# Hybrid attention trunk: deferred steps counted by written pieces, new ranks for PSUM copies and exponentials, later memory operands, and tiles moved from the raw ring to the temporaries

## The chip, the cores and the metric

The kernel runs on one core of a Trainium2 chip. The metric is the device time of one execution in microseconds; less is better. The time before is the median of 3 runs, 1416.64 us (1414.54 to 1416.74).

The engines are named as the profile names them: PE does the matmuls (PEld loads their weights), DVE, ACT and POOL do the elementwise work, SP issues all DMAs. Each works through its own instructions in a fixed order; semaphores tie them together.

## The reference

Two layers of an encoder over 512 tokens of width 1024. Each layer adds three parts to x:

```python
def hybrid_mixer(h, w_in, rpb, q_norm, k_norm, w_out, rows, cos, sin):
    proj = h @ w_in
    na_q, na_k, na_v, g_q, g_k, g_v = jnp.split(proj, IN_SPLIT_POINTS, axis=-1)
    na_out = neighbourhood_attention(...)                       # 8 heads of 64, window 8 x 16, learned bias
    g_q = apply_axial_rope(rms_norm(g_q, q_norm), cos, sin)     # 8 query heads
    g_k = apply_axial_rope(rms_norm(g_k, k_norm), cos, sin)     # 2 key heads
    gqa_out = gqa_block_attention(g_q, g_k, g_v)
    return jnp.concatenate([na_out, gqa_out], axis=-1) @ w_out

for l in range(DEPTH):
    x = x + hybrid_mixer(rms_norm(x, norm_mix[l]), ...)
    x = x + memory_cross_attention(rms_norm(x, ...), rms_norm(mem, ...), ...)   # 4 heads, 256 memory tokens
    x = x + conv_ffn(rms_norm(x, norm_ffn[l]), ...)             # width 2816, depthwise conv of 3, SwiGLU
return rms_norm(x, norm_final)
```

The parts that matter here are the grouped-query heads: their queries and keys are normalised per head and rotated before the scores.

## The kernel before, in words

**Precision and weights.** Every product is done in three matmuls of split operands (`mm3`): a high part hi, rounded to the matmul's type, and the rest lo. A weight tile is loaded by SP into a ring `raw` (`N_RAW`, 3 buffers of 512 KB in all), cast by ACT to hi (L260), and subtracted by POOL, seldom DVE, to lo (L261); hi and lo have 4 buffers each (`N_W`). `get_w` writes these steps: when weight n is asked for, the casts up to n + 2 and the loads up to `N_RAW` beyond the last cast are written. A load waits on SP, in SP's order, until the subtraction that frees its buffer is done.

**Order.** PE and SP keep the order in which the program is written. ACT, DVE and POOL are ordered before the run by a list scheduler: each instruction has a rank, the running number at which it was written; of what is ready in the scheduler's own estimate the lowest rank goes first. `behind(n)` adds n to the rank: positive goes later, negative earlier. On the chip these orders are fixed. A tile is taken from its pool when the scheduler places its first writer, and given back after its last reader; a writer waits until a buffer is free.

**Weaving.** In the mixer a hand-written pipeline (`weave`) runs the attention units: scores in slot s, softmax scaling in s + 1, transposes in s + 2, values after that. Between them a `Filler` writes pieces of projections. A piece is what a generator writes up to its next `yield`: half a projection (12 matmuls of 128x512), a quarter of the values, half an output block. The order of the fillers is: projections of the neighbourhood heads (`NA_ORDER`), then `gqa_project` for k, head pairs 0 and 1, v, head pairs 2 and 3 (two pieces each, p1 and p2), then `out_na`, `memory_keys`, `memory_values`, `close_rows`. A second filler, `ms`, prepares the memory operands; `MEM_STEPS[s]` says how many of its steps are written in slot s of the grouped-query attention. Its first step loads the memory (`load_mem`, two DMAs), later ones compute its statistics in layer 0 (squares L524, reductions L525, L532), and then its scaled and split operands (L508 POOL, L509 ACT, L510 POOL), which `memory_keys` reads.

**Deferred steps.** `late(n, fn)` holds back a step until n ticks have passed. `Late.tick` runs after each written piece (also of `ms`), and, before the change, also when a generator has ended (`Filler.step`). A step deferred from outside a tick counts one more, for the tick that follows at once. The steps that matter are these:

- `gqa_rope` after p2 of a head pair or of k: ACT copies the product out of PSUM (`xs`, L797) and squares it (`sq`, L798), DVE makes `cc` (L799).
- `swap`, one piece later: SP moves the halves of the head dimension by four DMAs into `xr`; PE sums the squares (`pv`); DVE (L808, L811) makes v.
- `rotate`, one piece after that: POOL takes the power (L817), spreads it to the head's columns (L818, into `sq`), and rotates (L819, L820).
- `norm`, two pieces later: PE turns the spread row factors (`mm<-ident,t` in the trace).
- `split`: DVE multiplies (L830), and `split_q` or `split_k` (L623 ACT, L627 DVE for k; L641, L643 for q) write the operands of the scores; for k, `double` then copies each half to the other partitions by SP.
- in layer 0, `project_first` defers `evict`: PE repeats the row factors of the first norm (`spread`, after the power L389 on POOL), ACT copies them (L399), and the first three projections are split.
- `straddle` (five DMAs of value blocks) and `turn` (transposes of the grouped values) are deferred likewise.

**Buffers.** PSUM has 4 tiles "mm" for products, 2 "sc" for scores, 2 "tr" for transposes and statistics. The pool `tpool` has 10 tiles `t` of 2 KB a partition for temporaries: exponentials (`es`, two a unit), `th` and `tt` of the values (L747, L748), `xs`, `xr`, `sq`, `cc`.

Of the kernel before, what the change touches and what calls it, by code (L numbers as in the profile page):

```python
# [12 lines left out]
AF = mybir.ActivationFunctionType  # L13
ALU = mybir.AluOpType
# [4 lines left out]
P = 128  # L19
# [5 lines left out]
NB = S // P  # L25
KC = D // P
HD = 64
# [6 lines left out]
BIG = 3.0e38  # L34
# [3 lines left out]
WTYPE = [0, 1, 1, 2]  # L38
# [9 lines left out]
NA_FILL = 2650  # L48
GQA_FILL = [2300] * 16 + [3000] * 4
MEM_FILL = [1, 1, 1, 2, 1, 0, 0, 2, 0, 1, 2]  # L50
MEM_STEPS = [1, 0, 1, 1, 1, 1, 1, 1, 1] + [0] * 11
W_BEHIND, N_RAW, N_W, AHEAD, AHEAD_HELD, N_WARM, N_LATE, N_FIRST = 45, 3, 4, 2, 5, 10, 4, 3


class InOrder:
# [67 lines left out]
class Filler:  # L123
# [9 lines left out]
    def step(self, n):  # L133
        while n > 0 and not self.closed():
            try:
                self.gate = next(self.gens[0])
                n -= 1
            except StopIteration:
                self.gens.pop(0)
            self.late.tick()  # L140

    def run(self, ns):
        self.owed += ns
# [29 lines left out]
def encoder_kernel(ctx: ExitStack, tc: tile.TileContext, t: dict, out: bass.AP):  # L173
    nc = tc.nc
    PE, SP = Counted(tc, nc.tensor), InOrder(tc, nc.sync)
    late = Late()
    ACT_IN_ORDER = InOrder(tc, nc.scalar)
    ACT, DVE, POOL = Free(nc.scalar), Free(nc.vector), Free(nc.gpsimd)
# [2 lines left out]
    xpool = ctx.enter_context(tc.tile_pool(name="xpool", bufs=1))  # L181
    wpool = ctx.enter_context(tc.tile_pool(name="wpool", bufs=N_W))
    rpool = ctx.enter_context(tc.tile_pool(name="rpool", bufs=22))
    tpool = ctx.enter_context(tc.tile_pool(name="tpool", bufs=10))
    spool = ctx.enter_context(tc.tile_pool(name="spool", bufs=24))
    psum = ctx.enter_context(tc.tile_pool(name="psum", bufs=2, space=PSUM))

    @contextmanager
    def behind(n):


        at = tc.cur_priority
        tc.cur_priority = at + n
        yield
        tc.cur_priority = at
# [177 lines left out]
    ident = cpool.tile([P, P], F32, name="ident")  # L373
# [182 lines left out]
    for l in range(DEPTH):  # L556
# [4 lines left out]
        bias = [None] * 4  # L561

        def load_bias(p):
            bias[p] = [rtile((4, 256), F32) for _ in range(2)]
            for j in range(2):
                SP.dma_start(bias[p][j][:, 0:3, :], t["bias"][l, 2 * p + j])
# [53 lines left out]
        def split_k(pm, kt, near):  # L620
            rows = [(slice(64 * j, 64 * j + 64), slice(64 - 64 * j, 128 - 64 * j)) for j in range(2)]
            for k, (r, o) in zip(kt, rows):
                ACT.copy(k[r, 0], pm[r])  # L623
                if near:
                    ACT.copy(k[o, 0], pm[r])
            for k, (r, o) in zip(kt, rows):
                DVE.tensor_sub(k[r, 1], pm[r], f(k[r, 0]))  # L627
                if near:
                    DVE.tensor_sub(k[o, 1], pm[r], f(k[r, 0]))

            def double():
                for k, (r, o) in zip(kt, rows):
                    SP.dma_start(f(k[o]), f(k[r]))

            if not near:
                late(2, double)

        def split_q(pm, st):
            halves = [(st[:, j], slice(64 * j, 64 * j + 64), slice(64 - 64 * j, 128 - 64 * j)) for j in range(2)]
            for v, r, o in halves:  # L640
                ACT.copy(v[r], pm[r])  # L641
            for v, r, o in halves:
                DVE.tensor_sub(v[o], pm[r], f(v[r]))  # L643
# [35 lines left out]
        def na_scores(u):  # L679
            p, bp = divmod(u, 2)  # L680
            if bp == 0 and p + 1 < 4:
                load_bias(p + 1)
            qst, kst = qk["q", p], qk["k", p]
            sc = [ps_s().rearrange("p (i n) -> p i n", i=2) for _ in range(2)]
            for i in range(2):
                b = 2 * bp + i
                qs, ks = slice(b * P, b * P + P), slice(WIN[b], WIN[b] + 256)
                for j in range(2):
                    for part in range(2):
                        PE.matmul(sc[j][:, i, :], qst[j][:, qs], kst[2 * part + j][:, ks], start=part == 0, stop=part == 1)  # L690
            nmx, sums = small(4), small(4)
            es = [tmp((2, 256)) for _ in range(2)]
            for j in range(2):
                for i in range(2):
                    b = 2 * bp + i
                    col = slice(2 * j + i, 2 * j + i + 1)
                    DVE.tensor_tensor_reduce(
                        out=sc[j][:, i, :], in0=sc[j][:, i, :], in1=bias[p][j][:, WTYPE[b], :],
                        op0=ALU.add, op1=ALU.min, scale=-1.0, scalar=BIG, accum_out=nmx[:, col])
            for j in range(2):  # L700
                for i in range(2):
                    col = slice(2 * j + i, 2 * j + i + 1)
                    ACT.activation(es[j][:, i, :], sc[j][:, i, :], AF.Exp, bias=nmx[:, col], scale=-1.0,
                                   accum_out=sums[:, col])
            na[u] = es, sums

        def na_normalise(u):
# [51 lines left out]
        gq, gk, gvt, gtab, r2 = [None] * 4, [], [], [], []  # L759
# [33 lines left out]
        def gqa_rope(g, pm):  # L793

            gain = qkg[:, l, 0:1] if g != "k" else qkg[:, l, 1:2]
            xs, xr, sq, cc = tmp(), tmp(), tmp(), tmp()
            ACT.activation(xs, pm, AF.Copy, scale=gain)  # L797
            ACT.activation(sq, pm, AF.Square)  # L798
            DVE.scalar_tensor_tensor(cc, pm, gain, gtab[0][:, 0], op0=ALU.mult, op1=ALU.mult)  # L799

            def swap():
                for i in range(4):
                    SP.dma_start(xr[32 * i : 32 * i + 32], xs[32 * (i ^ 1) : 32 * (i ^ 1) + 32])
                pv = ps_t()
                for b in range(NB):
                    PE.matmul(pv[:, 2 * b : 2 * b + 2], sq[:, b * P : (b + 1) * P], pairs, start=True, stop=True)
                v = small(2 * NB)
                DVE.tensor_tensor(v.rearrange("p (b j) -> p b j", j=2), pv[:, 0 : 2 * NB].rearrange("p (b j) -> p b j", j=2),  # L808
                                  r2[0].unsqueeze(2).to_broadcast([P, NB, 2]), op=ALU.mult)

                DVE.tensor_scalar(v, v, *((1.0 / HD, EPS) if g == "k" else (1.0, EPS * HD)), op0=ALU.mult, op1=ALU.add)  # L811
                late(1, lambda: rotate(v))

            def rotate(v):
                r = small(2 * NB)
                with behind(-40):
                    POOL.tensor_tensor(r, v, mhalf[:, : 2 * NB], op=ALU.pow)  # L817
                    POOL.tensor_copy(sq.rearrange("p (b d) -> p b d", d=HD), r.unsqueeze(2).to_broadcast([P, 2 * NB, HD]))  # L818
                POOL.tensor_mul(xr, xr, gtab[0][:, 1])  # L819
                POOL.tensor_add(xr, cc, xr)  # L820
                late(3, norm)

            def norm():
                pr = ps_mm()
                for b in range(NB):
                    PE.matmul(pr[:, b * P : (b + 1) * P], sq[:, b * P : (b + 1) * P], ident, start=True, stop=True)
                late(1, lambda: split(pr))

            def split(pr):
                DVE.tensor_mul(pr, xr, pr)  # L830
                if g == "k":
                    gk.extend(rtile((2, S)) for _ in range(2))
                    split_k(pr, gk, False)
                else:
                    gq[g] = rtile((2, S))
                    split_q(pr, gq[g])

            late(2, swap)


        ga, gpt = {}, {}
# [146 lines left out]
        def na_quanta(s):  # L988
# [324 lines left out]
```

## Time and profile before

| | |
|---|---|
| median of 3 runs | 1416.64 us |
| profiled execution, its own time | 1417.6 us |
| its span, first to last instruction | 1415.8 us |
| mean granted PE clock | 0.987 |
| DMA: bytes, mean rate | 138.83 MB, 98 GB/s |
| SP waiting for POOL's lo (L261) | 1031.8 us, 193 times |

The profile is one execution. "Busy" is the time in which an engine had an instruction running. Lines such as "[3.54 <-DVE r L627]" mean that the engine was idle for 3.54 us before the instruction, and that the last thing it waited for was DVE's instruction of line 627 that writes an r tile. The granted clock is the share of full speed at which PE was let run. Line numbers are those of the kernel before. Between about 370 us and 690 us, and between about 1060 us and 1360 us, the kernel is in the feed-forward part of a layer.

### The profile page before, as it was taken

The numbers are of one execution on the slowest core, as the hardware profiler recorded it, in microseconds if no ns is written. First come the engines' busy times: TensorE is split into PE (matmuls) and PEld (weight loads), VectorE is DVE, ScalarE is ACT, GpSimd is POOL, SyncE is SP. The second block draws the span as 40 slices with busy tenths as digits, with TensorE's granted clock in tenths as the row PEclk, the third lists the DMA queues.
The fourth block names the chain that finished last, engine by engine and source line by source line (L and its number), as shares of the span: only waits on it lengthen the run. The fifth ranks groups of instructions, "written<-read, shape, count | busy, mean of one in ns | idle before, by whom it ended". The sixth has DMA issues, their size and how long they took to land. (4 is left out here: it accounts for less than half of the span.)

```text
span 1415.8 us, 19240 instructions
## 1 busy us (share of the span) xinstructions
PE 1364.5 (96%) x7092; PEld 1165.1 (82%) x7092; DVE 838.2 (59%) x1421; ACT 703.2 (50%) x1308; POOL 724.0 (51%) x541
## 2 busy tenths in 40 slices
PE   7998899999999999999999988999999999999997
PEld 6897789877888888888888866997788888888897
DVE  4665876454687178358446555744638843871874
ACT  5675677655443234234556655766555432432341
POOL 2357866734444444444635767657164444444452
PEclk8999999999999999999999999999999999999998
DMA  7552412322333333332446431223133333333221
GB/s 233 145 151 72 114 46 75 104 74 61 89 95 100 103 90 93 102 96 87 135 130 172 126 96 47 63 73 114 37 96 95 93 104 89 100 93 105 88 77 60
DMA packets 218174, 138.83 MB, mean 98 GB/s; under 512 B 5984, under 2 KB 211040, under 8 KB 218080
## 3 DMA queue, kind: packets, MB, share of 16 engines
q1 hardware_dynamic: 218080, 137.60, 34.1%
q8 instruction: 56, 0.92, 0.3%
q14 instruction: 38, 0.31, 0.1%
HBM read 125.00 MB, written 2.10 MB: 90 GB/s over the span
## 5 line engine op out<-in xcount | busy, mean ns | idle before, releaser
L261 POOL TENSOR_TENSOR lo<-raw,hi 128x1024 fp32r<-128x1024 f32 (+2 forms) x268 | 499.1, 1874 | 517.4 <-ACT hi L260 497.8
L76 PE MATMUL mm<-xg,hi 128*128 128x512 f32 x1984 | 620.1, 394 | 9.0 <-DVE r L627 7.1
L76 PEld LDWEIGHTS mm<-xg,hi 128*128 128x128 f32 x1984 | 371.2, 189 | 85.1 <-issue 7.4
L260 ACT CAST hi<-raw 128x512 fp32r<-128x512 f32 (+2 forms) x276 | 224.1, 836 | 339.2 <-PE mm L76 285.3
L76 PE MATMUL mm<-xg,lo 128*128 128x512 f32 x992 | 388.4, 392 | 0.0
L76 PE MATMUL mm<-r,hi 128*128 128x512 f32 (+1 forms) x1160 | 337.0, 374 | 2.7 <-DVE r L457 2.0
L76 PEld LDWEIGHTS mm<-r,hi 128*128 128x128 f32 x1160 | 210.8, 189 | 41.2 <-DVE r L457 2.8
L1137 DVE SCALAR_TENSOR_TENSOR t<-t,par,t 128x7 f32<-128x7 f32 (+1 forms) x352 | 203.8, 646 | 34.0 <-ACT t L1130 34.0
L76 PEld LDWEIGHTS mm<-xg,lo 128*128 128x128 f32 x992 | 187.9, 189 | 40.0 <-DVE lo L261 0.4
L76 PE MATMUL mm<-r,lo 128*128 128x512 f32 (+1 forms) x580 | 216.5, 373 | 0.0
L76 PEld LDWEIGHTS mm<-r,lo 128*128 128x128 f32 x580 | 109.6, 189 | 19.3
L463 POOL TENSOR_SCALAR t<-t,s 128x512 f32<-128x512 f32 (+1 forms) x112 | 66.9, 613 | 77.3 <-DVE s L863 35.6
L1122 DVE TENSOR_TENSOR t<-mm,rep 128x512 f32<-128x512 f32 x88 | 60.1, 687 | 77.3 <-PE mm L76 62.0
L1139 ACT ACTIVATE t<-t 128x512 f32<-128x512 f32 x44 | 27.9, 633 | 139.2 <-DVE t L1137 139.1
L1143 DVE TENSOR_TENSOR r<-t,r 128x512 fp32r<-128x512 f32 x44 | 90.5, 2057 | 7.4 <-ACT r L1142 4.3
L1166 DVE TENSOR_TENSOR xT<-xT,mm 128x512 f32<-128x512 f32 x32 | 21.9, 686 | 106.7 <-PE mm L76 106.7
L76 PE MATMUL sc<-r,r 128*128 128x256 f32 (+1 forms) x352 | 72.5, 337 | 3.6 <-DVE r L457 1.7
L63 PE MATMUL tr<-ident,t 128*128 128x128 f32 x456 | 63.1, 277 | 6.1 <-DVE s L532 1.8
L1130 ACT ACTIVATE t<-t,par 128x512 f32<-128x512 f32 x88 | 66.8, 806 | 2.4 <-DVE t L1122 2.4
L63 PEld LDWEIGHTS tr<-ident,t 128*128 128x128 f32 x456 | 53.9, 143 | 13.5 <-issue 4.1
L76 PE MATMUL mm<-r,r 128*128 128x256 f32 (+1 forms) x428 | 62.4, 298 | 0.0
L76 PEld LDWEIGHTS sc<-r,r 128*128 128x128 f32 x352 | 52.0, 192 | 9.9 <-ACT r L456 3.0
(134 smaller groups left out, 1544.7 us busy)
## 6 DMA issues: line engine op xcount, KB each, us to landing
raw<-in_w_up SPq DMA_DIRECT2D x88, 512.0 KB, 3.9
raw<-in_w_in SPq DMA_DIRECT2D x34, 512.0 KB, 5.2
raw<-in_w_down SPq DMA_DIRECT2D x32, 448.0 KB, 3.8
raw<-in_w_mem_kv SPq DMA_DIRECT2D x16, 512.0 KB, 4.1
raw<-in_w_down SPq DMA_DIRECT2D x16, 512.0 KB, 4.2
r<-in_bias SPq DMA_DIRECT2D x16, 384.0 KB, 6.2
r<-r SPq DMA_DIRECT2D x22, 256.0 KB, 4.1
raw<-in_w_out SPq DMA_DIRECT2D x8, 512.0 KB, 5.0
```

Source lines behind the costliest of these rows:

```text
L63: return lambda *a, **k: self.tc.keep_in_program_order(op(*a, **k))
L76: return self.tc.keep_in_program_order(self.engine.matmul(out, lhsT, rhs, **k))
L260: act.copy(hi[:, k], raw[:, k])
L261: (POOL if eng[0] == "P" else DVE).tensor_sub(lo[:, k], raw[:, k], f(hi)[:, k])
L463: eng.tensor_scalar(e, e, sums[:, col : col + 1], 1.0, op0=ALU.mult, op1=ALU.mult)
L1122: DVE.tensor_mul(u, us[side], ffn.rep)
L1130: ACT.activation(cc, u, AF.Identity, bias=par[:, l, CB + ch : CB + ch + 1], scale=w[1])
L1137: DVE.scalar_tensor_tensor(cc[:, dst], u[:, src], wi, cc[:, dst], op0=ALU.mult, op1=ALU.add)
L1139: ACT.activation(cs[0], cs[0], AF.Silu)
L1143: DVE.tensor_sub(acts[j][1], cs[0], f(acts[j][0]))
L1166: DVE.tensor_add(xT[m], xT[m], pm)
```

## The change

Six things are done.

- `Filler.step` ticks only when a piece was written, no longer when a generator has ended. The delays of the rotation are set anew: swap 2 to 1, norm 3 to 2. The other deferred steps keep their numbers.
- The three instructions that read the product in `gqa_rope` get a rank 20 lower (earlier).
- The reductions and exponentials of the neighbourhood scores get a rank 30 higher (later).
- `xr` is taken in `swap` and not in `gqa_rope`; the spread row factors get a tile of their own, `rows`, in `rotate`, and no longer overwrite `sq`.
- `tpool` has 12 tiles and not 10; the raw ring has 2 buffers and not 3.
- `MEM_STEPS` starts two slots later.

```diff
-MEM_STEPS = [1, 0, 1, 1, 1, 1, 1, 1, 1] + [0] * 11
-W_BEHIND, N_RAW, N_W, AHEAD, AHEAD_HELD, N_WARM, N_LATE, N_FIRST = 45, 3, 4, 2, 5, 10, 4, 3
+MEM_STEPS = [0, 0, 1, 0, 1, 1, 1, 1, 1, 1, 1] + [0] * 9
+W_BEHIND, N_RAW, N_W, AHEAD, AHEAD_HELD, N_WARM, N_LATE, N_FIRST = 45, 2, 4, 2, 5, 10, 4, 3
...
                 self.gate = next(self.gens[0])
                 n -= 1
+                self.late.tick()
             except StopIteration:
                 self.gens.pop(0)
-            self.late.tick()
...
-    tpool = ctx.enter_context(tc.tile_pool(name="tpool", bufs=10))
+    tpool = ctx.enter_context(tc.tile_pool(name="tpool", bufs=12))
...
             es = [tmp((2, 256)) for _ in range(2)]
+            with behind(30):
...
-            xs, xr, sq, cc = tmp(), tmp(), tmp(), tmp()
-            ACT.activation(xs, pm, AF.Copy, scale=gain)
-            ACT.activation(sq, pm, AF.Square)
-            DVE.scalar_tensor_tensor(cc, pm, gain, gtab[0][:, 0], op0=ALU.mult, op1=ALU.mult)
+            xs, sq, cc = tmp(), tmp(), tmp()
+            with behind(-20):
+                ACT.activation(xs, pm, AF.Copy, scale=gain)
+                ACT.activation(sq, pm, AF.Square)
+                DVE.scalar_tensor_tensor(cc, pm, gain, gtab[0][:, 0], op0=ALU.mult, op1=ALU.mult)
 
             def swap():
+                xr = tmp()
...
-                late(1, lambda: rotate(v))
+                late(1, lambda: rotate(xr, v))
 
-            def rotate(v):
+            def rotate(xr, v):
                 r = small(2 * NB)
+                rows = tmp()
                 with behind(-40):
                     POOL.tensor_tensor(r, v, mhalf[:, : 2 * NB], op=ALU.pow)
-                    POOL.tensor_copy(sq.rearrange("p (b d) -> p b d", d=HD), r.unsqueeze(2).to_broadcast([P, 2 * NB, HD]))
+                    POOL.tensor_copy(rows.rearrange("p (b d) -> p b d", d=HD), r.unsqueeze(2).to_broadcast([P, 2 * NB, HD]))
                 POOL.tensor_mul(xr, xr, gtab[0][:, 1])
                 POOL.tensor_add(xr, cc, xr)
-                late(3, norm)
+                late(2, lambda: norm(xr, rows))
...
-                    PE.matmul(pr[:, b * P : (b + 1) * P], sq[:, b * P : (b + 1) * P], ident, start=True, stop=True)
-                late(1, lambda: split(pr))
+                    PE.matmul(pr[:, b * P : (b + 1) * P], rows[:, b * P : (b + 1) * P], ident, start=True, stop=True)
+                late(1, lambda: split(xr, pr))
...
-            late(2, swap)
+            late(1, swap)
```

In `na_scores` the reductions and exponentials are only indented under `with behind(30)`; the rest of their code is the same.

More of the change, by code (lines that the diff above doesn't have):

```diff
@@ L692, in na_scores @@
             es = [tmp((2, 256)) for _ in range(2)]
[L693 to L704, printed above, removed]
+            with behind(30):
+                for j in range(2):
+                    for i in range(2):
+                        b = 2 * bp + i
+                        col = slice(2 * j + i, 2 * j + i + 1)
+                        DVE.tensor_tensor_reduce(
+                            out=sc[j][:, i, :], in0=sc[j][:, i, :], in1=bias[p][j][:, WTYPE[b], :],
+                            op0=ALU.add, op1=ALU.min, scale=-1.0, scalar=BIG, accum_out=nmx[:, col])
+                for j in range(2):
+                    for i in range(2):
+                        col = slice(2 * j + i, 2 * j + i + 1)
+                        ACT.activation(es[j][:, i, :], sc[j][:, i, :], AF.Exp, bias=nmx[:, col], scale=-1.0,
+                                       accum_out=sums[:, col])
             na[u] = es, sums
@@ L811, in swap, with norm, split @@
                 DVE.tensor_scalar(v, v, *((1.0 / HD, EPS) if g == "k" else (1.0, EPS * HD)), op0=ALU.mult, op1=ALU.add)
-                late(1, lambda: rotate(v))
-            def rotate(v):
+                late(1, lambda: rotate(xr, v))
+            def rotate(xr, v):
                 r = small(2 * NB)
+                rows = tmp()
                 with behind(-40):
                     POOL.tensor_tensor(r, v, mhalf[:, : 2 * NB], op=ALU.pow)
-                    POOL.tensor_copy(sq.rearrange("p (b d) -> p b d", d=HD), r.unsqueeze(2).to_broadcast([P, 2 * NB, HD]))
+                    POOL.tensor_copy(rows.rearrange("p (b d) -> p b d", d=HD), r.unsqueeze(2).to_broadcast([P, 2 * NB, HD]))
                 POOL.tensor_mul(xr, xr, gtab[0][:, 1])
                 POOL.tensor_add(xr, cc, xr)
-                late(3, norm)
-            def norm():
+                late(2, lambda: norm(xr, rows))
+            def norm(xr, rows):
                 pr = ps_mm()
                 for b in range(NB):
-                    PE.matmul(pr[:, b * P : (b + 1) * P], sq[:, b * P : (b + 1) * P], ident, start=True, stop=True)
-                late(1, lambda: split(pr))
-            def split(pr):
+                    PE.matmul(pr[:, b * P : (b + 1) * P], rows[:, b * P : (b + 1) * P], ident, start=True, stop=True)
+                late(1, lambda: split(xr, pr))
+            def split(xr, pr):
                 DVE.tensor_mul(pr, xr, pr)
```

## The prediction

> **What bounds the kernel now.** I read the page first, then the busy time by stretches, then what the tensor engine waited for, then the timeline of each engine around its longest waits.
>
> ```profile
> span 1415.8 us, 19240 instructions
> ```
> ```profile
> PE 1364.5 (96%) x7092; PEld 1165.1 (82%) x7092; DVE 838.2 (59%) x1421; ACT 703.2 (50%) x1308; POOL 724.0 (51%) x541
> ```
>
> PE is busy for 96% of the span. The change adds and removes no matmul, so it can win only inside the other 51.3 us and in time lost to a lower clock. The stretches (busy us of PE, PEld, DVE, ACT, POOL, then granted clock, DMA share, GB/s) say where that lies:
>
> ```profile
> 125.00:175.00 50.00, 41.26 (x221) 35.14 (x219) 34.93 (x54) 28.42 (x56) 38.20 (x43) 0.93 0.33 90
> 800.00:875.00 75.00, 61.39 (x323) 51.62 (x323) 41.13 (x82) 40.83 (x93) 56.84 (x62) 0.93 0.29 80
> 400.00:425.00 25.00, 25.00 (x112) 20.72 (x111) 20.61 (x26) 10.55 (x14) 10.77 (x6) 1.00 0.33 94
> ```
>
> The feed-forward part (third row) has no idle PE at all: 25.00 us for 112 matmuls, 0.223 us each. The two stretches where the grouped-query heads are projected, rotated and normalised, one per layer, lose 8.7 and 13.6 us to idle PE, and their clock of 0.93 costs about 0.07 x 50 + 0.07 x 75 = 8.8 us more. PE's waits (total us, times, longest) name the causes:
>
> ```profile
> PE mm L76 <- POOL t L818: 7.4, 3, 3.9
> PE mm L76 <- DVE r L627: 7.1, 2, 3.5
> PE tr L76 <- POOL s L389: 6.9, 4, 4.4
> PE tr L76 <- ACT t L798: 5.5, 4, 2.3
> ...
> PE tr L63 <- DVE s L532: 1.8, 1, 1.8
> ...
> PE tr L63 <- DVE xg L457: 1.8, 2, 1.2
> ```
>
> Every one of these except part of L389 belongs to a step that the change moves or ranks anew. I call the two pieces of a projection p1 and p2 (12 matmuls, 12 x 0.223 = 2.7 us each).
>
> **The change part by part.**
>
> *The counter.* Before, the end of a generator also ticks. A projection spans two pieces and one such end, so a delay that crosses an end is a piece shorter than it reads. The new delays (swap 2 to 1, norm 3 to 2) put swap and norm back where they were. What was not re-tuned really moves, by one piece: the first evict, split (delay 1 from norm), double and straddle (copies through SP), the turn of the values. Steps of the memory filler tick as well, so the first slot of the grouped heads loses one tick, and the norm of head pair 2 falls one piece (six matmuls) later.
>
> *Evict in layer 0* (term 1). It now runs before the first piece of the next projection:
>
> ```profile
> 32.38 2.08 PE L76 MATMUL tr<-ident,s 128*128 128x128 f32 x8 [4.36 <-POOL s L389]
> ```
> ```profile
> 44.24 1.12 PE L76 MATMUL sc<-r,r 128*128 128x256 f32 x8
> ```
> ```profile
> 26.39 4.95 POOL L261 TENSOR_TENSOR lo<-raw,hi 128x512 fp32r<-128x512 f32 x4 [5.30 <-ACT hi L260]
> 31.30 1.04 POOL L389 TENSOR_TENSOR s<-s,mhalf 128x4 f32<-128x4 f32 x1
> ```
> ```profile
> 41.57 0.69 DVE L629 TENSOR_TENSOR r<-mm,r 64x512 fp32r<-64x512 f32 x1
> ```
>
> PE stands still from 28.0 to 32.4 because the power on POOL sits behind four weight subtractions. After, p1 (2.7 us) fills that hole and the repeat follows it at 30.7 at the earliest. But the first scores then wait for the splits, which end 42.26 - 32.38 = 9.9 us after the repeat starts: 40.6 at the earliest instead of 44.24, a gain of 3.6; if POOL keeps its order, the repeat stays at 32.38 and the scores start at 42.3, a gain of 1.9. I take **3.0**, nearer the first, since with one raw buffer less the later of those subtractions come later than the power.
>
> *Split of k, and copies in front* (terms 2 and 3). At 129.07 PE wants a buffer of the "mm" ring (4) for the values' projection:
>
> ```profile
> 129.07 0.70 PE L76 MATMUL mm<-xg,hi 128*128 128x512 f32 x2 [3.54 <-DVE r L627]
> ```
> ```profile
> 123.84 1.15 ACT L260 CAST hi<-raw 128x512 fp32r<-128x512 f32 x2
> 124.87 0.53 ACT L715 ACTIVATE t<-t,s 128x256 f32<-128x256 f32 x1
> 125.28 0.69 ACT L797 ACTIVATE t<-mm,qkg 128x512 f32<-128x512 f32 x1
> 125.85 0.61 ACT L798 ACTIVATE t<-mm 128x512 f32<-128x512 f32 x1
> 126.33 1.17 ACT L623 CAST r<-mm 64x512 fp32r<-64x512 f32 x2
> 135.02 1.19 ACT L747 COPY t<-mm 64x512 f32<-64x512 f32 x2 [7.52 <-PE tr L63]
> ```
> ```profile
> 127.53 1.39 DVE L627 TENSOR_TENSOR r<-mm,r 64x512 fp32r<-64x512 f32 x2 [2.15 <-ACT r L623]
> 128.95 0.75 DVE L799 SCALAR_TENSOR_TENSOR t<-mm,qkg,r 128x512 f32<-128x512 f32 x1
> ```
>
> All four are held: by the product of head pair 1 (until L799, 129.7), by the row factors of k (until L627, 128.9), and by two value products whose copy L747 starts only at 135.02. After, L797 to L799 rank in front of L260 and can end near 123.84 + 0.7 + 0.6 + 0.75 = 125.9, and L799 is no longer queued behind k's split, which comes a piece later. PE, ready at 129.07 - 3.54 = 125.5, would stand 0.5 us with a semaphore's time instead of 3.54. Two layers: 7.1 - 1.0 = **6.1**, between 0 and 7.1. The cast put behind costs nothing as long as the weight buffers lead (below).
>
> The four waits on L798 (5.5 us) are the swap's matmuls arriving before the square, behind a cast of the weights. The two longest, one a layer, follow a projection with only the first scores between:
>
> ```profile
> 157.73 1.05 PE L76 MATMUL tr<-pairs,t 128*128 128x2 f32 x8 [1.79 <-ACT t L798]
> ```
> ```profile
> 847.08 1.05 PE L76 MATMUL tr<-pairs,t 128*128 128x2 f32 x8 [2.29 <-ACT t L798]
> ```
> ```profile
> 844.69 1.13 ACT L260 CAST hi<-raw 128x512 fp32r<-128x512 f32 x2
> ```
>
> Without the casts ahead, 1.13 each, 0.66 and 1.16 are left of them; the other two, 1.4 together, vanish: 5.5 - 1.8 = **3.7**. The exponentials ranked behind wait only where ACT has something else; their rows are read two slots later, some 20 us, which hides it.
>
> *Memory two slots later, own tile for the rows* (terms 4 and 5).
>
> ```profile
> 164.60 1.87 POOL L508 TENSOR_SCALAR r<-r,par 128x256 f32<-128x256 f32 x4
> 166.39 0.63 POOL L818 COPY t<-s 128x512 f32<-128x512 f32 x1
> ```
> ```profile
> 167.08 1.76 PE L76 MATMUL mm<-ident,t 128*128 128x128 f32 x8 [2.29 <-POOL t L818]
> ```
> ```profile
> 860.28 0.62 POOL L818 COPY t<-s 128x512 f32<-128x512 f32 x1
> ```
>
> POOL runs the memory's scaling (L508, four for 1.87 us, eight a layer) ahead of the copy L818 that PE waits for. Loaded two slots later, the memory is not there yet. Of the three waits I leave 0.4 each on two: 7.4 - 0.8 = **6.6**, between 2 and 7.4. The waits on L532 (the memory's own statistics) and on L457, 3.6 us, move to later slots with the work; I count half, **1.8**, between 0 and 3.6. The moved step takes its two loads past one weight load on SP, its squares and reductions to slots 4 and 5. It is needed here:
>
> ```profile
> 213.62 0.40 PE L76 MATMUL mm<-r,hi 128*128 128x256 f32 x2
> ```
>
> That is slot 10; the last operands are written in slot 9, one slot (5.5 us) before, so there is cover, but little.
>
> *Tiles of tmp, 10 to 12, later taken.* At 125 us the code wants 16 tiles before: 4 of exponentials, 3 of values, 2 of k, 3 of head pair 0, 4 of pair 1. After, k's rows are already free and pair 1 has no tile for the swap yet: 14. Where tiles lack, SP waits too:
>
> ```profile
> SPq L63 <- DVE t L748: 43.3, 5, 15.7
> ```
>
> I read this as the swap's DMAs standing up to 15.7 us for a tile that the values still hold, with raw loads and doublings behind them in the same queue. This is what keeps terms 2 and 4 from failing; I give it no time of its own.
>
> *Raw buffers 3 to 2, doubling and straddle a piece later* (price nothing). In the feed-forward part:
>
> ```profile
> 500.99 2.41 POOL L261 TENSOR_TENSOR lo<-raw,hi 128x1024 fp32r<-128x1024 f32 x1 [3.06 <-ACT hi L260]
> ```
> ```profile
> 510.74 1.05 ACT L260 CAST hi<-raw 128x1024 fp32r<-128x1024 f32 x1 [2.84 <-PE mm L76]
> ```
> ```profile
> raw<-in_w_up SPq DMA_DIRECT2D x88, 512.0 KB, 3.9
> ```
>
> The load that goes out when a subtraction ends (503.4) lands at 507.3. With three buffers it serves the third cast after, with two the second, at 510.74: 3.4 us to spare, and PE is three weights further behind. The doubling of k goes out one piece and one weight load later, some 5 us, and is read two projections later. Straddle and the other doublings pass no weight load, since that piece is a second half.
>
> *Clock* (term 6). Fewer and shorter holes give back most of the 8.8 us: **7.0**, between 0 and 8.8.
>
> [...]
>
> *Sum.* 3.0 + 6.1 + 3.7 + 6.6 + 1.8 + 7.0 = 28.2 us. Against it I set new waits: without L508's 3.7 us POOL has 34.5 us of work in some 41 us of the first stretch and 53.1 in some 64 of the second, 84% and 83% of an engine that works in a fixed order. Ten projections are left with a wait each; I take 0.8 us, a little over the mean of the residues above (0.5, 0.66, 1.16, 0.4), so 8 us. 28.2 - 8 = 20.2. The profiled execution took 1417.6 us (span 1415.8 and 1.8 around it): 1397.4; it lay 1.0 above the median of the runs, 1416.64, so I say **1397** for the runs.
>
> **The rivals.**
>
> *Tiles still bind.* 14 wanted is above 12, and the rows now need a tile of their own. For: L747 waited 7.52 us although ACT was free. Against: 6 short becomes 2 short. Terms 2, 3, 4 and 6 halve: 28.2 - 11.7 - 8 = 8.5 us, 1408 (1404 to 1414).
>
> *Nothing is given back.* The full 28.2: about 1388 (1381 to 1389). Against it, the 84%.
>
> *The change does not do what it says.* Ranks and delays only order instructions before the run; if each queue comes out in an order with the same last arrivals, the time is 1414 to 1419. Against it: at least evict and split move in PE's own order.
>
> *Slower: the raw ring starves.* Two buffers turn over in landing + cast + subtraction, L + 1.05 + 2.41 + 0.1; two weights last PE 2 x 24 x 0.223 = 10.7 us. From L = 7.1 us on, PE waits at every weight. At L = 8 it is 0.4 us for each of 136 weights, 54 us, less the 20 above: about 1450; in a mild form 1420 to 1450. For: the ring is the only thing that the change makes smaller. Against: L is 3.9.
>
> **How the numbers follow.** Forecast (1389 to 1404) 0.50; tiles bind 0.22; nothing given back 0.10; no effect 0.07; slower 0.11. A measurement of this kernel tells about 0.2%, 2.8 us, from no change. Faster by more: 0.50 + 0.22 + 0.10 = 0.82; within: 0.07; slower: 0.11. Leaving out the slower case, the unchanged one and the lowest end of the third case, the range is 1384 to 1414; the likeliest case alone has 1389 to 1404.
>
> **What would show it.** PE's wait on L627 gone or below 1 us each; the wait on L818 gone with no L508 before 175 us; the wait on L798 down to two of about 1 us; scores at 44.24 some 3 us earlier; clock 0.97 or more in both stretches; no PE wait on a weight's hi or lo, and 25.00 us of PE in the feed-forward rows. A wait on L818 of 2 us or more says that tiles bind. PE waiting for lo anywhere after the start, or a feed-forward row below 25.00, says that the raw ring was the price. New waits on the transposes' tiles in slots 4 to 9 would say that the memory only moved its waits.

## The result, and the profile after

The kernel after takes **1402.39 us** (median of 4 runs, 1401.19 to 1403.34); the kernel before took 1416.69 us on the same chip (4 runs). The ratio is 0.9899, 95% interval 0.9882 to 0.9916: faster by 14.3 us. The forecast was 1397 us, 1384 to 1414. The profiled execution took 1401.19 us, the lowest of the four, so the profiles differ by a little more than the medians: their spans by 1415.8 - 1399.2 = 16.6 us.

Line numbers from L747 on shift a little. The rotation's copy, square and cc (before L797 to L799) are L799 to L801; v (L808, L811) is L811, L814; power, spread and rotation (L817 to L820) are L821 to L824; the multiply L830 is L834; the values' copy L747 is L748 and their L748 is L749; the grouped exponential L857 is L861; the reciprocal L863 is L867.

From the page of after:

```profile
span 1399.2 us, 19213 instructions
```
```profile
PE 1358.8 (97%) x7092; PEld 1158.8 (83%) x7092; DVE 835.1 (60%) x1421; ACT 702.8 (50%) x1308; POOL 722.9 (52%) x541
```

PE's idle time fell from 51.3 to 1399.2 - 1358.8 = 40.4 us. Its busy time fell too, by 5.7 us for the same 7092 matmuls; the mean clock rose from 0.987 to 0.993, and I count the 5.7 us as its share. The stretches of after, with the columns of the prediction:

```profile
0.00:50.00 50.00, 45.60 (x245) 38.92 (x246) 29.92 (x56) 31.99 (x61) 15.29 (x20) 0.97 0.66 194
125.00:175.00 50.00, 42.98 (x242) 35.60 (x241) 35.74 (x61) 28.78 (x57) 35.97 (x38) 1.00 0.37 100
800.00:875.00 75.00, 68.64 (x383) 59.05 (x383) 48.66 (x93) 45.74 (x103) 57.64 (x65) 0.95 0.30 85
```
```profile
400.00:425.00 25.00, 25.00 (x112) 20.69 (x111) 21.41 (x28) 11.21 (x15) 11.39 (x5) 1.00 0.32 93
```

The stretches are fixed in time, so after has got further in each. The clock is 1.00 in the first mixer stretch (0.93 before) and 0.95 in the second; in the first 50 us PE is busy for 45.60 us (before: 42.37, at a clock of 0.90). The feed-forward row is full, as before. PE's waits of after (total us, times, longest):

```profile
PE tr L63 <- DVE r L457: 3.8, 2, 1.9
PE mm L76 <- DVE t L801: 2.9, 2, 1.4
PE tr L76 <- ACT t L800: 2.7, 2, 1.3
PE tr L76 <- POOL s L389: 2.5, 3, 1.0
PE tr L63 <- DVE xg L457: 2.3, 2, 1.7
...
PE tr L63 <- POOL r L508: 1.6, 1, 1.6
PE mm L76 <- DVE r L643: 1.4, 1, 1.4
...
PE tr L63 <- ACT mem_rep L539: 0.8, 1, 0.8
```

The wait on the spread copies (L818 before, 7.4 us) is gone, and so is that on k's split (L627, 7.1); in its place stands 2.9 on cc. The waits on the power L389 and on the square lost 4.4 and 2.8. The waits on the transposes' tiles (`tr L63`) have grown: 6.1 us on L457 where there were 1.8, and 2.4 on the memory's own L508 and L539 where there were 1.8 on L532.

### The profile page after: what moved, and what is told of

Same layout as the page of the kernel before. It is cut to its first block, busy times and chain, and to the rows that moved or that the text cites. A ratio compares the mean times of both kernels' runs of the same rounds, so it can differ in the third digit from the quotient of the medians.

```text
span 1399.2 us, 19213 instructions
## 1 busy us (share of the span) xinstructions
PE 1358.8 (97%) x7092; PEld 1158.8 (83%) x7092; DVE 835.1 (60%) x1421; ACT 702.8 (50%) x1308; POOL 722.9 (52%) x541
## 4 chain that ended last, share of the span: by engine, by line
PE 88%; DVE 4%; ACT 3%; issue 2%; POOL 1%; DMA 1%; SPq 0%; DVEq 0%; ACTq 0%; POOLq 0%
PE mm L76 80%; PE sc L76 3%; PE tr L63 3%; PE tr L76 1%; ACT hi L260 1%; DVE r L457 1%; DMA raw<-in_w_down 1%; POOL lo L261 0%; POOL r L261 0%; DVE xg L457 0%; DMA raw<-in_w_in 0%; DVE s L859 0%; ACT t L800 0%; ACT t L799 0%; DVE t L801 0%
## 5 line engine op out<-in xcount | busy, mean ns | idle before, releaser
L261 POOL TENSOR_TENSOR lo<-raw,hi 128x1024 fp32r<-128x1024 f32 (+2 forms) x268 | 499.6, 1876 | 507.9 <-ACT hi L260 476.3
L76 PE MATMUL mm<-xg,hi 128*128 128x512 f32 x1984 | 617.7, 393 | 4.3 <-DVE t L801 2.9
L76 PEld LDWEIGHTS mm<-xg,hi 128*128 128x128 f32 x1984 | 369.9, 189 | 80.1 <-DVE t L801 3.3
L260 ACT CAST hi<-raw 128x512 fp32r<-128x512 f32 (+2 forms) x276 | 224.5, 836 | 347.0 <-PE mm L76 288.4
L76 PE MATMUL mm<-xg,lo 128*128 128x512 f32 x992 | 387.7, 391 | 0.0
L76 PE MATMUL mm<-r,hi 128*128 128x512 f32 (+1 forms) x1160 | 336.1, 374 | 2.5 <-DVE r L457 2.0
L76 PEld LDWEIGHTS mm<-r,hi 128*128 128x128 f32 x1160 | 210.3, 189 | 41.2 <-DVE r L457 2.8
L76 PEld LDWEIGHTS mm<-xg,lo 128*128 128x128 f32 x992 | 187.1, 189 | 40.3 <-DVE lo L261 0.7
L76 PE MATMUL mm<-r,lo 128*128 128x512 f32 (+1 forms) x580 | 216.1, 373 | 0.0
L76 PEld LDWEIGHTS mm<-r,lo 128*128 128x128 f32 x580 | 109.3, 188 | 19.2
L463 POOL TENSOR_SCALAR t<-t,s 128x512 f32<-128x512 f32 (+1 forms) x112 | 66.3, 607 | 75.2 <-DVE s L710 38.2
L76 PE MATMUL sc<-r,r 128*128 128x256 f32 (+1 forms) x352 | 73.2, 339 | 4.4 <-DVE r L457 1.8
L63 PE MATMUL tr<-ident,t 128*128 128x128 f32 x456 | 62.8, 274 | 11.8 <-DVE r L457 3.8
L63 PEld LDWEIGHTS tr<-ident,t 128*128 128x128 f32 x456 | 52.4, 140 | 20.4 <-issue 7.9
L76 PE MATMUL mm<-r,r 128*128 128x256 f32 (+1 forms) x428 | 62.5, 297 | 0.1
L76 PEld LDWEIGHTS sc<-r,r 128*128 128x128 f32 x352 | 51.8, 191 | 10.6 <-ACT r L456 3.0
```

The costliest lines, as they stand in the source:

```text
L63: return lambda *a, **k: self.tc.keep_in_program_order(op(*a, **k))
L76: return self.tc.keep_in_program_order(self.engine.matmul(out, lhsT, rhs, **k))
L260: act.copy(hi[:, k], raw[:, k])
L261: (POOL if eng[0] == "P" else DVE).tensor_sub(lo[:, k], raw[:, k], f(hi)[:, k])
L463: eng.tensor_scalar(e, e, sums[:, col : col + 1], 1.0, op0=ALU.mult, op1=ALU.mult)
```

## The experiments

The runs below come from several chips, and each ratio is to runs of the kernel before on the same chip (medians 1416.18 to 1418.93 us). Two variants of after are told apart by their ratios only from about 0.003 on; where the text uses less, it is the place of a wait in the traces that decides.

### The parts alone, added to the kernel before

**Tiles** (with the smaller raw ring, as in after).

```diff
-... N_RAW ... = 45, 3, 4, ...      tpool bufs=10
+... N_RAW ... = 45, 2, 4, ...      tpool bufs=12
```

> The kernel before with 12 temporary tiles and 2 raw buffers, nothing else. My theory (tiles): the hole of 3.54 us ahead of the values' projection shrinks to about 1.4 us in both layers and part of the clock comes back, the waits on L818 stay: 7 us less, ratio 0.995 (0.993 to 0.997). Rival (the raw ring has a price): PE or the casts wait for weights, and the gain is eaten: 0.998 or more. Rival (order): the hole is set by the place of k's split and stays at 3.5 us: 0.998 to 1.002.

1407.74 us, ratio 0.9932 [0.9916, 0.9947]: 9.3 us, two thirds of the whole gain, with no rank, delay or step changed; the ring's own share is in the next run. The hole before the values' projection, 3.54 us in before, in this run:

```profile
125.48 0.73 PE L76 MATMUL mm<-xg,hi 128*128 128x512 f32 x2 [1.67 <-DVE t L799]
```

k's split no longer ends it; PE waits only until DVE has read the product of head pair 1. The copy of the value products, which started at 135.02 in before after 7.52 us of idle ACT, and SP's wait on the values' tiles, 43.3 us in before, are in this run:

```profile
126.04 1.19 ACT L747 COPY t<-mm 64x512 f32<-64x512 f32 x2
```
```profile
SPq L63 <- DVE t L748: 0.8, 2, 0.5
```

**The raw ring.**

```diff
-... N_RAW ... = 45, 3, 4, ...
+... N_RAW ... = 45, 2, 4, ...
```

> The kernel before with one edit: N_RAW 3 to 2 (the raw weight ring alone, 10 temporaries as before). It prices what the slower rival of the prediction blamed. Theory: the ring costs nothing, because a load lands in 3.9 us and the subtraction that frees the buffer runs well ahead of PE; 1415 to 1419 us, ratio 0.999 to 1.001, feed-forward windows at 25.00 us of PE. Rival: the ring has a price of its own, which the two more temporaries only paid back in the earlier runs; then 3 us or more over the kernel before, ratio 1.002 or more, with PE waits on lo or hi, or loads later in the mixer.

1417.51 us (12 runs; the profiled one, 1413.19, is the lowest), ratio 1.0011 [0.9999, 1.0022]. The smaller ring costs at most 0.2%. One PE wait on a weight shows, 0.7 us on a cast 5.2 us into the run; with three buffers e8_evict has one of 0.3 us. SP's wait on the values' tiles (L748) is 43.0 us here, so it is the tiles and not the ring that end it in e6_tmp12. POOL at the start, in this run:

```profile
26.27 2.50 POOL L261 TENSOR_TENSOR lo<-raw,hi 128x512 fp32r<-128x512 f32 x2 [5.54 <-ACT hi L260]
28.74 1.02 POOL L389 TENSOR_TENSOR s<-s,mhalf 128x4 f32<-128x4 f32 x1
```

Before, four subtractions (4.95 us) stood ahead of the power; now two do, and it starts 2.6 us earlier. That is what term 1 supposed. The first scores start at 39.15 here, 5.1 us earlier than in before, and yet the median is no lower: an earlier start of the scores need not reach the end of the run.

**Evict.**

```diff
-            late(1, evict)
+            late(2, evict)
```

> The kernel before with the first evict of layer 0 one piece later, as the new counter puts it, nothing else. My theory: p1 of the next projection fills the hole of 4.36 us at 28 us, the first scores come at about 40 instead of 44.2: 4 to 5 us less, ratio 0.9968 (0.996 to 0.998). Rival: the scores wait for the splits in any case and POOL's power keeps its place behind the subtractions: 2 us or less, 0.9985 to 1.0.

1414.76 us, ratio 0.9981 [0.9973, 0.999]: 2.3 to 2.7 us. The first scores start at 40.49 instead of 44.24; of these 3.75 us not all is left at the end.

**Memory.**

```diff
-MEM_STEPS = [1, 0, 1, 1, 1, 1, 1, 1, 1] + [0] * 11
+MEM_STEPS = [0, 0, 1, 0, 1, 1, 1, 1, 1, 1, 1] + [0] * 9
```

> The kernel before with the memory's steps two slots later, nothing else. My theory: L508 no longer stands ahead of L818, the three holes of 7.4 us shrink to under 1.5 us with some 3 us of clock, and new holes of about 3 us come in slots 2 to 5: 6 us less, ratio 0.9955 (0.993 to 0.998). Rival (the run with the old slots read as the memory being everything): 14 us less, 0.990.

1412.21 us, ratio 0.9961 [0.9949, 0.9974]: 4.8 to 5.5 us. POOL here (compare L508 at 164.60 and L818 at 166.39 in before):

```profile
164.02 0.62 POOL L818 COPY t<-s 128x512 f32<-128x512 f32 x1
170.59 3.67 POOL L508 TENSOR_SCALAR r<-r,par 128x256 f32<-128x256 f32 x8 [2.88 <-ACT r L524]
```

The two changed places, and PE's waits on L818 fell from 7.4 to 0.2 us. New waits on the grouped exponentials (L857) came, 4.4 us in all.

### The parts undone, in the kernel after

**Memory steps as before.**

```diff
-MEM_STEPS = [0, 0, 1, 0, 1, 1, 1, 1, 1, 1, 1] + [0] * 9
+MEM_STEPS = [1, 0, 1, 1, 1, 1, 1, 1, 1] + [0] * 11
```

> The changed kernel with the memory's steps in their old slots. My theory: POOL's scaling L508 comes back ahead of the spread of the row factors, the wait on it returns (up to 7.4 us, with 2 to 4 us of clock), while the holes that the later memory made in slots 2 to 5 (1.66, 0.70, 0.65, 0.83 and 1.69 us) go: 1402.4 + 10 - 5.5 = 1407 us (1404 to 1410). Rival: the wait on the spread was for tiles, and the own tile for the rows with 12 tiles cured it; the time stays within 1.5 us of 1402.4, or falls by the 5.5 us to 1397.

1416.7 us, ratio 0.9989 [0.9978, 1.0]: almost all of the gain is gone. What I expected, L818's waits back in both layers, is wrong for layer 0 (one of 2.2 us came back, in layer 1). Most of the loss is one hole, in the memory's own statistics:

```profile
163.55 0.40 PE L76 MATMUL mm<-r,lo 128*128 128x512 f32 x1
175.15 0.99 PE L76 MATMUL tr<-ones,t 128*128 128x1 f32 x4 [11.20 <-DVE s L867]
```
```profile
163.35 2.00 ACT L524 ACTIVATE r<-r 128x1024 f32<-128x1024 f32 x2
```
```profile
165.51 1.94 DVE L525 TENSOR_REDUCE t<-r 128x256 f32<-128x1024 f32 x1
167.36 0.68 DVE L859 TENSOR_REDUCE s<-sc 128x1 f32<-128x512 f32 x1
167.96 1.93 DVE L525 TENSOR_REDUCE t<-r 128x256 f32<-128x1024 f32 x1
169.81 0.68 DVE L457 TENSOR_TENSOR xg<-tr,xg 128x512 fp32r<-128x512 f32 x1
...
171.61 3.39 DVE L526 TENSOR_TENSOR t<-t 128x256 f32<-128x256 f32 x1
```

PE is at its statistics step at 163.95, while ACT has only begun the squares; reductions and sum follow until 175.0. (The wait is put down to L867, a short reciprocal that DVE runs right behind the sum; what PE's step reads is the sum L526.) In before, the same PE step stood at 172.88, without a wait, since PE itself was late:

```profile
172.88 0.50 PE L76 MATMUL tr<-ones,t 128*128 128x1 f32 x4
```

So the other parts bring PE to that point about 9 us earlier, and the memory must move out of the way, or it takes all back. Alone, the new steps are worth 5 us; in company, between the two ratios (0.9989 and 0.9899), 13.

**Counter and delays as before.**

```diff
+            self.late.tick()        # again after a generator's end
-                late(2, lambda: norm(xr, rows))
+                late(3, lambda: norm(xr, rows))
-            late(1, swap)
+            late(2, swap)
```

> The changed kernel with the old counter (ticks at the end of a generator too) and the old delays of swap and norm; ranks, tiles, memory stay as changed. My theory: the evict of layer 0 stands again ahead of the next piece (5.4 us lost), the split of k again ahead of the values' projection (1 to 2 us a layer lost), the turn is back in its good place (3.8 us won): 1402.4 + 5.4 + 3 - 3.8 = 1407 us (1405 to 1410), with the hole of about 4 us at 30 us back. Rival: the two tiles more did it and the counter only renumbers: 1399 to 1403.

1402.52 us, ratio 0.9885 [0.9868, 0.9901]: as fast as after. Evict's hole returns (3.37 us on L389, scores at 42.8), but the turn of the values goes back to its place, and both 1.9-us waits on L457 go. The hole before the values stays at 1.4 us twice, though k's split is back in its old place: the split's place did not make it.

**The turn a piece earlier.**

```diff
-            late(2, turn)
+            late(1, turn)
```

> The changed kernel with the delay of the values' turn set from 2 to 1, where it stood before the counter changed. My theory: what the counter moved without a new number can also land badly; the turn now comes right ahead of the transposes of the last unit, takes one of the two tr tiles, and costs PE one hole of 1.90 us in layer 0 (140.46) and one of 1.91 us in layer 1 (825.94). Both go, the rest stays: 1402.4 - 3.8 = 1398.6 us (1397 to 1400). Rival: the tr tiles are short in any order there, and the hole only moves to the next user of them: 1401.5 to 1403.

1400.86 us, ratio 0.9878 [0.986, 0.9897]. The turn takes one of the two "tr" tiles. A piece later, in after, it stands right ahead of the last attention unit's transposes, which need both; the second of them (140.46) waits until DVE has read the turn's tile (136.63):

```profile
136.63 0.60 PE L63 MATMUL tr<-ident,t 128*128 128x128 f32 x4
137.07 1.06 PE L76 MATMUL mm<-ident,t 128*128 128x128 f32 x8
137.96 0.60 PE L63 MATMUL tr<-ident,t 128*128 128x128 f32 x4
140.46 0.63 PE L63 MATMUL tr<-ident,t 128*128 128x128 f32 x4 [1.90 <-DVE r L457]
```

Both such holes are gone here. In place of the 3.8 us, the waits on the square grow from 1.33 to 1.7 us each, and another wait on L457 from 0.6 to 1.5. The median is 1.5 us lower (0.002 of the ratio), less than the runs can tell.

**Ranks at 0.**

```diff
-with behind(30): ...   with behind(-20): ...
+with behind(0): ...    with behind(0): ...
```

> The changed kernel with both new ranks at 0 (copies out of PSUM not in front, exponentials not behind). My theory: the ranks do nearly nothing, since in the trace after the cast L260 still runs ahead of L799 at 118.05 and 148.27, because the product is not ready when ACT comes free: 1402.4 within 1.5 us, and PE's wait on L800 stays at about 2.7 us. Rival (terms 2 and 3 of the prediction): the ranks shortened the waits on the square (5.5 to 2.7 us) and on the product's buffer (7.1 to 2.9 us); without them 1406 to 1409.

1401.16 us, ratio 0.9881 [0.9865, 0.9897]: the ranks do nothing that can be measured in the time. In the trace they do a little: without them PE waits on the square (L800) four times, 4.4 us in all, against twice and 2.7 in after; its span is no longer for that (1398.3 against 1399.2). ACT in after shows why it is not more, with both ranks set:

```profile
118.05 1.14 ACT L260 CAST hi<-raw 128x512 fp32r<-128x512 f32 x2
119.08 0.70 ACT L799 ACTIVATE t<-mm,qkg 128x512 f32<-128x512 f32 x1
119.66 0.61 ACT L800 ACTIVATE t<-mm 128x512 f32<-128x512 f32 x1
120.14 0.53 ACT L716 ACTIVATE t<-t,s 128x256 f32<-128x256 f32 x1
120.54 1.17 ACT L623 CAST r<-mm 64x512 fp32r<-64x512 f32 x2
121.73 1.19 ACT L748 COPY t<-mm 64x512 f32<-64x512 f32 x2
```

The cast L260 still runs ahead of the copy. By the code, the scheduler takes the lowest rank of what is ready, and the cast is ready before the product is: a rank chooses among what is ready, and can't hold an engine free. That reason is read from the order, not tried by itself.

**Ten tiles.**

```diff
-tpool bufs=12
+tpool bufs=10
```

> The changed kernel with 10 temporary tiles instead of 12 (the raw ring stays at 2). My theory by now: with the old counter and without the ranks PE's hole ahead of the values' projection stayed at 1.4 us, so it is the tiles that shortened it from 3.54; with 10 tiles it goes back to about 3.5 us in both layers, SP's wait on the values' tiles (43 us before) returns, the clock falls again: about 7 us more, a ratio to the kernel before of 0.995 (0.993 to 0.998). Rival: taking xr later and the rows' own tile already cured it: 0.989 to 0.991 as with 12.

1404.07 us, ratio 0.991 [0.9895, 0.9925]. The hole before the values is 2.4 and 1.8 us instead of 1.4 twice. By the ratios two tiles fewer cost after some 1.6 us, which the runs hardly tell from nothing, where two more gave the kernel before 9.3: something else in after does most of their work. It shows in SP's wait on the values' tiles too (L749 in this kernel): 14.8 us with ten tiles here, 43.0 with ten in e9_raw2. Ranks and counter, undone one at a time, are worth nothing, and the later memory alone leaves the hole as it was (7.7 us on L627 in e7_mem). So the later `xr`, with the own tile for the rows, is what is left for that; it was not run alone, and neither were the parts undone together.

### Towards a better version

**Old counter, evict moved by hand.** The kernel of e4_oldcount with evict two ticks late:

```diff
-            late(1, evict)
+            late(2, evict)
```

> The kernel after, with the old counter (a tick at a generator's end too, swap 2 and norm 3 as before) and evict deferred by 2 instead of 1, so that evict alone stands a piece later and the turn of the values, split and doubling stand where they stood in the kernel before. Theory: the counter's only useful effect was evict (first scores at 38.8 us instead of 42.8 us) and its only harm the turn; the other two parts add up, so 1402.5 - 4.0 = 1398.5 us, ratio 0.986 to 0.9875, no wait of 1.5 us or more on L457 in slots 1 and 2 of the grouped heads. Rival: an earlier arrival at the grouped heads meets the memory's and the swap's chains again, and half or more of the 4.0 us comes back as new waits there; then 1400.5 us or more, ratio 0.9885 or more.

1401.48 us, ratio 0.9898 [0.9885, 0.9911]. The scores start at 38.7, 4.1 us earlier than in e4_oldcount. At the end of the two traces 2.7 us of that are left (spans 1398.0 and 1400.7), and between the runs nothing that can be told: the median is 1.0 us lower, the ratio no better (0.9885 there; the chips differ). The time is the rival's.

**Swap a piece later.** The kernel after with:

```diff
-            late(2, turn)      late(1, swap)
+            late(1, turn)      late(2, swap)
```

> The kernel after, with turn deferred by 1 (as in the run e1_turn) and swap deferred by 2 in the new count, so that the swap's matmuls come one written piece later than in both kernels. Theory: the waits of PE on the square (L800, 1.7 us twice in e1_turn) and on the value v (L811, about 1 us) are only arrivals too early by less than a piece of 2.7 us, so they go and nothing else comes: 1400.9 - 4 = 1397 us, ratio 0.985 to 0.9865. Rival: with the swap later, the copies and squares keep their tiles a piece longer and the split comes a piece later, so that PE waits on the mm ring or on the transposes' tiles instead; then 1400 us or more, ratio 0.9875 or more, with new waits on L801, L832 to L834 or L749.

1403.7 us, ratio 0.9915 [0.9902, 0.9928]. The waits on cc (L801) are down to 0.7 us and those on the square to 1.0, in all. But PE's waits now read:

```profile
PE mm L76 <- POOL t L822: 9.1, 4, 3.4
PE tr L63 <- DVE xg L457: 3.8, 2, 2.6
```

POOL's spread copy, the step after v, is the late one. The rival was right on the time; of the waits that it named, those on the transposes' tiles grew (L457, from 2.3 us in e1_turn), but the largest is on L822, which it did not name.

**Swap and norm a piece later.** The kernel of e11_swap with:

```diff
-                late(2, lambda: norm(xr, rows))
+                late(3, lambda: norm(xr, rows))
```

> The kernel of e11_swap (after, turn deferred by 1, swap by 2) with norm deferred by 3 instead of 2, so that the whole rotation stands a written piece later than in after. In e11_swap the waits on the square and on v were gone (first segment after k's swap without idle time), but PE waited 9.1 us in four waits on POOL's spread copies L822. Theory: what is late in the rotation is the chain swap, square, v, power, spread as a whole, and each step is bought with one more piece in front of PE's step that reads it; a piece of 2.7 us before norm cuts the waits of 1.14, 3.43, 1.14 and 3.44 us to at most about 0.8 each for the two long ones and none for the short ones, some 7.5 us, so 1403.7 - 7.5 = 1396 us, ratio 0.984 to 0.987. Rival: the wait moves on once more, to the split that the scores read, or to the mm ring and the transposes' tiles; then 1400 us or more, ratio 0.9885 or more, with waits of over 2 us on L801, L832 to L834, L643 or L749.

1400.12 us, ratio 0.9879 [0.986, 0.9898]. Two of the four waits on L822 are left, 5.5 us, and 2.9 us on the memory's statistics (L867) are new, and those on L643 have grown from 1.4 to 4.4. POOL in layer 1, while PE waits until 846.3:

```profile
842.60 1.30 POOL L824 TENSOR_TENSOR t<-t,t 128x512 f32<-128x512 f32 x1
843.84 1.87 POOL L508 TENSOR_SCALAR r<-r,par 128x256 f32<-128x256 f32 x4
845.62 0.65 POOL L822 COPY t<-s 128x512 f32<-128x512 f32 x1
```

That is the picture from which the change set out: the memory's scaling ahead of the copy. Six versions (after, e1_turn, e2_noranks, e4_oldcount, e10_best, e12_swap_norm) lie between 1400.1 and 1402.5 us with intervals that overlap; none is shown to beat after.

## Why the prediction was right, and where its steps were wrong

Sign and size held: 20.2 us forecast on the profile, 16.6 measured on it, 14.3 between the medians. That the size came so near is in part luck: the part that is worth most alone, the tiles, was given no time, what it won was booked on ranks and order, and the 8 us given back were an estimate whose reason did not hold. The waits of PE give the account (after less before, us): L389 -4.4, L627 to L801 -4.2, square -2.8, spread copy -7.4, together -18.8; all other waits +7.9; idle time -10.9. With the 5.7 of busy time that is 16.6.

**Term 1, evict (3.0): right mechanism, more at the scores than said and less at the end.** The repeat starts at 30.67 as supposed, and the scores at 38.81, 5.4 us earlier. Not 9.9 but 8.1 us lie between them; I count a part of that as the clock, granted at 1.00 from 30.67 to 38.81 here and at 0.73 from 32.38 to 42.26 in before. The repeat and what PE waits for next:

```profile
30.67 1.05 PE L76 MATMUL tr<-ident,s 128*128 128x128 f32 x8
```
```profile
35.86 0.36 PE L76 MATMUL mm<-hi,xg 128*128 128x256 f32 x1 [1.39 <-DVE r L643]
```

The repeat takes 1.05 us where it took 2.08 behind the 4.36-us hole. Evict and the shorter ring each do part of it (e8_evict, e9_raw2). Alone, evict is worth 2.3 to 2.7 us of the whole time and the ring nothing that shows, so the 5.4 us at the scores are not a gain of 5.4.

**Terms 2 and 3, copies in front and k's split (9.8): the step that failed.** 7.0 us were won, but not by "L797 to L799 rank in front of L260": where the wait stood, they don't, and ranks and split's place are worth nothing in the time (e2_noranks, e4_oldcount). Most of it is the tiles' (in e6_tmp12 the same waits fall by 5.5 us). I had read SP's wait of 43.3 us on the values' tiles and the late copy L747 (135.02) rightly, and then gave the tiles "no time of its own". They are the largest part by themselves: the copy starts at 126.04 with the tiles alone and at 121.73 in after, and that frees the products' buffers in time.

**Term 4, spread copy (6.6): the waits went (7.4), by another order than I said.** "No L508 before 175 us" did not hold:

```profile
156.89 0.62 POOL L822 COPY t<-s 128x512 f32<-128x512 f32 x1
...
162.51 3.67 POOL L508 TENSOR_SCALAR r<-r,par 128x256 f32<-128x256 f32 x8 [2.41 <-ACT r L524]
```

The memory's scaling stands where it stood (164.60 before); the copy comes 9.5 us earlier (166.39 before), ahead of it. Two slots later in program order is nearly no later in time, when all else runs ahead by that much. The parts overlap here: of the 7.4 us, 0.2 are left with the memory's steps alone (e7_mem), 4.1 with the tiles and the ring (e6_tmp12), 3.5 with the ring alone (e9_raw2), and with all but the memory's steps 2.2 come back (e3_mem_old).

**Term 5, the memory's own waits (+1.8): wrong sign.** They and L457's grew from 3.6 to 8.5 us. 3.8 of that is the turn, which I listed among what moves by a piece and did not follow to its tiles. The sentence on "new waits on the transposes' tiles" names what came, for the memory's part of it.

**Term 6, clock (7.0): about right.** 5.7 us of busy time. The second stretch reached 0.95, short of the 0.97 that was to show it.

**The give-back (8):** with term 5, about the right size, for a reason that the traces of after don't bear out. All waits outside terms 1 to 4 grew by 7.9 us, term 5's 4.9 among them; for the two together the sum had 8 - 1.8 = 6.2. But POOL, which was to be 84% and 83% busy, is at 72% and 77% in the two stretches and ends only 1.6 us of the new waits (L508); most of the rest ends on DVE, at the "tr" tiles. (The 64 us behind the 83% don't follow from the prediction's own rows either: 75 - 13.6 is 61.4, which gives 86%.) POOL comes next: pushed further (e11_swap, e12_swap_norm), the waits land on L822.

**The rivals.** The raw ring does not starve PE: the feed-forward row is at 25.00 and the ring alone is within 0.2% (e9_raw2). That tiles would still bind at 12 came true at most in part: SP's wait on the values' tiles is down to 1.0 us in after, but among the swap's DMAs SP waits 18.1 us, one wait a layer, until PE has read a tile (`tr L76`). Whether PE loses by that is open, since more than 12 tiles were not run.

## What to carry to other kernels

When an engine at 97% shows several waits that end on different lines, ask first which pool those lines share: here two more tiles did alone most of what ranks and order were credited with. A part's worth depends on what stands beside it (the memory steps: 5 us alone, 13 in company), so price it both by adding it and by undoing it. A count that is changed moves everything that hangs on it: follow each of those steps to the buffer that it takes, as the turn shows.

## What the runs showed of the hardware

**The clock after holes of the same length: lower in one layer, full in the other.** The same hole of 1.33 us stands in both layers of after:

```profile
150.66 1.05 PE L76 MATMUL tr<-pairs,t 128*128 128x2 f32 x8 [1.33 <-ACT t L800]
...
153.04 1.05 PE L76 MATMUL mm<-ident,t 128*128 128x128 f32 x8
```
```profile
837.74 1.05 PE L76 MATMUL tr<-pairs,t 128*128 128x2 f32 x8 [1.33 <-ACT t L800]
...
840.14 1.91 PE L76 MATMUL mm<-ident,t 128*128 128x128 f32 x8
841.71 1.99 PE L76 MATMUL sc<-r,r 128*128 128x512 f32 x4
843.54 0.62 PE L76 MATMUL mm<-r,hi 128*128 128x512 f32 x2
```

In layer 0 the eight matmuls that follow take 1.05 us, in layer 1 1.91: 2.4 us after the hole's end PE is slower there, for 3.4 us (840.14 to 843.54). The granted clock of 840.0 to 843.5 is 0.51; that of 153.0 to 156.5 in layer 0 is 1.00. The holes at the turn are such a pair too: 1.90 us at 140.46, with a clock of 1.00 from 140.0 to 143.5, and 1.91 us at 825.94, with 0.56 from 826.0 to 829.8. What decides between the layers was not tried.

**DVE beside POOL.** The sum L526 of two operands took 3.39 us in e3_mem_old (above) and 0.56 in after:

```profile
172.52 0.56 DVE L526 TENSOR_TENSOR t<-t 128x256 f32<-128x256 f32 x1
```

In e3_mem_old POOL ran beside it, in this row and, until 171.99, in two weight subtractions (L261):

```profile
171.95 2.77 POOL L510 TENSOR_TENSOR r<-r,r 128x256 fp32r<-128x256 f32 x4
```

The sum ended at 175.0, just after POOL's four subtractions (174.7). In e12_swap_norm POOL stood idle beside it, from 172.98 until its next instruction at 174.42, and the sum took 0.41 us:

```profile
173.83 0.41 DVE L526 TENSOR_TENSOR t<-t 128x256 f32<-128x256 f32 x1
```
```profile
174.42 0.69 POOL L463 TENSOR_SCALAR t<-t,s 128x512 f32<-128x512 f32 x1 [1.44 <-DVE s L867]
```

POOL was not idle in after: its scaling L463 ran from 172.10 to 173.64. In before the sum took 1.08 us, next to POOL's addition L820 of two operands (168.79 to 170.08). These rows come from kernels that differ in other things too; no run changed POOL's work alone, and what makes the sum's time differ was not shown.
